# First steps of a one-core decoder layer: x loaded over two queues, squares on two engines, rows scaled in quarters, first casts on GpSimd, four small loads on another queue

## The chip, the core and the metric

The kernel runs on one core of one Trainium2 chip. The metric is the device time of one execution in microseconds (us); the median of the runs is compared. Engines are named as in the profile: PE (TensorE matmuls), PEld (its weight loads), DVE (VectorE), ACT (ScalarE), POOL (GpSimd) and SP (SyncE, which here only starts DMA transfers; its queue is SPq). Line numbers L... are those of the kernel before, unless the text says that they are the changed kernel's.

## What is computed

One decoder layer on x of 256 positions by 1024 channels, in float32. Only the first lines matter here: the row norm of x and the one projection that feeds both mixing branches.

```
def rms_norm(x, g):
    y = xf * lax.rsqrt(jnp.mean(xf * xf, axis=-1, keepdims=True) + NORM_EPS)
    return (y * g.astype(jnp.float32)).astype(x.dtype)
...
        h = rms_norm(x, norm1_g[l])
        proj = h @ w_in[l]
        z_rwkv = proj[..., :RWKV_IN]
...
        z_rwkv = z_rwkv + rwkv_mu[l] * (shift_right(z_rwkv) - z_rwkv)
        y_a = rwkv7_time_mix(z_rwkv, w_decay_up[l], decay_bias[l], w_aaa_up[l], aaa_bias[l],
...
        x = x + (g_a * u_a + g_b * u_b) @ w_out[l]
        h2 = rms_norm(x, norm2_g[l])
        x = x + conv_ffn(h2, w_ffn_up[l], ffn_conv_w[l], ffn_conv_b[l], w_ffn_down[l])
```

After the projection come an RWKV-7 branch (a recurrence over the positions) and a softmax attention branch, gates, an output projection and a gated MLP.

## The kernel before

Every product is made in three passes of float32r halves: an operand is split into a high part (a cast to float32r) and a low part (what the cast lost), and high times high, high times low and low times high are added up. For the activations these halves are `hh` and `hl`, for the weights `whi` and `wlo`. Weights come in pieces of 512 KB (128 partitions by 1024 float32) through `load_next`, which starts a DMA on SP's queue into one of four `raw` buffers (the first piece as two halves of 256 KB, the third piece only 128 KB); `split_hi` casts, `split_lo` subtracts and then starts the next load. Four more pieces are loaded ahead into two tiles named `early`. All DMAs that SP or ACT start share eight completion semaphores in turn, so the ninth waits for the first to land before it is started.

`first_steps` (L364) is written out by hand: within it PE, ACT, DVE and Pool run their instructions in the order of the text, while SP's queue is ordered by the scheduler; after it a scheduler orders all engines. Its order is this:

- x, two blocks of 128 rows in halves of 512 columns, is loaded by four DMAs on SP's queue (`load_x`, L81, called at L99), then come five issues for the first four weight pieces and four for the `early` tiles. ACT starts the load of `p0`, the eight rows of norm1_g.
- Eight dummy matmuls (`keep_warm`) run on PE meanwhile. Pool builds the identity matrix and starts eleven of the fifteen small loads (`small_loads`): ten fill the 51 rows of `p1` (rwkv_mu in two loads, decay_bias, aaa_bias, k_k, k_a, r_k, ln_g, ln_b, norm2_g), the eleventh and twelfth are the two halves of `wdu` (w_decay_up and w_aaa_up, 128 KB each), and the last three are gqk (two loads of 32 KB) and the positions. In the profile norm1_g and norm2_g are both shown as `in_norm_g`, and `p0` and `p1` both as `p`.
- For each row block t: ACT squares both halves with a row sum (L396), DVE scales the first sum and adds the epsilon (L399), ACT takes the root (L401), DVE the reciprocal (L402), and the halves are scaled (L408 on DVE; the last half on ACT, L406). PE transposes eight 128x128 tiles per block (L414); between the blocks four dummy matmuls run.
- The first weight piece is cast half by DVE (L432) and half by Pool (L433), and Pool subtracts (L437). ACT makes `hh` out of the transposes (`high`, L419), DVE makes `hl` (`low`, L422), for K = 0 to 7.
- The first projection's 48 matmuls (L461) run in an order of K and pass written out below; then `late_params` transposes `p1` on PE (L158), copies it to `par` on DVE (L159) and derives `omm` from it (L160). ACT's `shift` (L490) of the first projection needs `omm`, and a `tanh` of its result feeds the decay projection (L566), which uses `wdu`.

Behind that the generator `wst` runs the further projections with the matmuls of L302, L304 and L307.

Of the kernel before, what the change touches and what calls it, by code (L numbers as in the profile page):

```python
# [13 lines left out]
OP = mybir.AluOpType  # L14
# [23 lines left out]
def body(tc, x, positions, norm1_g, w_in, rwkv_mu, w_decay_up, decay_bias, w_aaa_up,  # L38
# [5 lines left out]
    with ctx:  # L44
# [36 lines left out]
        def load_x():  # L81
            xs = []
            for t in range(2):
                xt = b4("x").rearrange("p a b -> p (a b)")
                for cs in (slice(0, 512), slice(512, 1024)):
                    nc.sync.dma_start(xt[:, cs], xr[t * 128:(t + 1) * 128, cs])
                xs.append(xt)
            return xs
# [9 lines left out]

        x_sb = load_x()  # L99
# [84 lines left out]
        def small_loads(n):  # L184
            for _ in range(n):
                nc.gpsimd.dma_start(*loads.pop(0))
# [177 lines left out]
        def first_steps():  # L364

            for i in range(NRAW):
# [8 lines left out]
            nc.scalar.dma_start(p0, rows(norm1_g, 8))  # L377
# [4 lines left out]
            small_loads(11)  # L382
# [10 lines left out]
            for t in range(2):  # L393
                xn = [b2("xn1", [128, 512]) for _ in range(2)]
                for hf in range(2):
                    act.activation(xn[hf], x_sb[t][:, hf * 512:hf * 512 + 512], AF.Square,  # L396
                                   accum_out=ss[:, t, hf:hf + 1])
                    if hf == 0:
                        dve.tensor_scalar(ss[:, t, 0:1], ss[:, t, 0:1], 1.0 / D, NORM_EPS,  # L399
                                          op0=OP.mult, op1=OP.add)  # L400
                act.activation(rs[:, t:t + 1], ss[:, t, 1:2], AF.Sqrt, scale=1.0 / D, bias=ss[:, t, 0:1])  # L401
                dve.reciprocal(rs[:, t:t + 1], rs[:, t:t + 1])  # L402
                for hf in range(2):
                    src = x_sb[t][:, hf * 512:hf * 512 + 512]
                    if t and hf:
                        act.activation(xn[hf], src, AF.Copy, scale=rs[:, t:t + 1])  # L406
                    else:
                        dve.tensor_scalar(xn[hf], src, rs[:, t:t + 1], None, op0=OP.mult)  # L408
                if t == 0:
                    pe.transpose(pt[:, 0:8], p0, ident[:8, :8])  # L410
                    keep_warm(3)
                    dve.tensor_copy(par[:, 0:8], pt[:, 0:8])
                for k in range(8):
                    pe.transpose(at(k)[:, t], xn[k // 4][:, k % 4 * 128:k % 4 * 128 + 128], ident)  # L414
# [961 lines left out]
```

## Time and profile before

| what | value |
|---|---|
| median of 3 runs (lowest, highest) | 406.03 us (405.90, 407.27) |
| span of the profiled execution | 403.9 us |
| median above that span | 2.1 us |
| PE busy | 396.4 us, 98% of the span |
| DVE, ACT, POOL busy | 324.6, 233.9, 41.8 us |
| DMA moved | 70.53 MB, mean 175 GB/s |

The span is from the first to the last instruction of the one execution that was profiled; for that execution no time beside the span is recorded, so the 2.1 us are the distance between it and the median of the other runs. A row of the timeline has the start and the length in us, the engine, the line, the operation, the tiles written and read, the shape and the count of merged instructions; behind it in brackets stands how long the engine sat idle before it and what ended that. A DMA row has the transfer, the issuing queue, the count, KB each and the us from issue to landing. `x4` behind a row means that four instructions were merged, and its length is that of all of them.

### The profile page before, as it was taken

How to read it: one execution, taken by the hardware profiler on the slowest of the kernel's cores; microseconds unless marked ns; L12 is line 12 of the kernel's file. 1: busy time of each engine (PE TensorE's matmuls, PEld its weight loads, DVE VectorE, ACT ScalarE, POOL GpSimd, SP SyncE). 2: the span in 40 equal slices, each digit the busy share in tenths (PEclk: the TensorE clock that was granted, in tenths of full speed). 3: DMA queues.
4: the chain of work that ended last, by engine and by line, in shares of the span. 5: the costliest groups of instructions: out<-in, count | busy, mean ns of one | idle time of the engine just before them, and what ended most of it. 6: DMA issues, size and time to landing. Idle time of an engine off the chain costs nothing.

```text
span 403.9 us, 8280 instructions
## 1 busy us (share of the span) xinstructions
PE 396.4 (98%) x3250; PEld 348.7 (86%) x3250; DVE 324.6 (80%) x574; ACT 233.9 (58%) x397; POOL 41.8 (10%) x69
## 2 busy tenths in 40 slices
PE   7999999999989999999999999999999999999996
PEld 3999989788989989999888888888888888888885
DVE  3988999899667978778965898977869778687694
ACT  6799755475647676444563784655546446355440
POOL 7910070010500011020011000000000000000000
PEclk9999999999999999999999999999999999999999
DMA  8954555564783444536563756676665665656612
GB/s 243 317 168 154 160 161 158 160 176 150 159 220 104 115 150 131 183 112 207 191 183 97 242 157 208 181 232 189 200 204 163 208 187 177 207 174 209 196 48 104
DMA packets 61990, 70.53 MB, mean 175 GB/s; under 512 B 9421, under 2 KB 52243, under 8 KB 61952
## 3 DMA queue, kind: packets, MB, share of 16 engines
q1 hardware_dynamic: 61104, 69.54, 57.1%
q0 software_dynamic: 832, 0.47, 0.6%
q8 instruction: 25, 0.41, 0.5%
q14 instruction: 13, 0.11, 0.1%
q10 hardware_dynamic: 16, 0.00, 0.0%
HBM read 68.56 MB, written 1.44 MB: 173 GB/s over the span
## 4 chain that ended last, share of the span: by engine, by line
PE 93%; DVE 2%; ACT 1%; DMA 1%; issue 1%; SPq 0%; POOL 0%; DVEq 0%; POOLq 0%; ACTq 0%
PE acc L1262 15%; PE acc L302 9%; PE acc L304 8%; PE acc L307 8%; PE acc L1267 8%; PE at L1262 5%; PE acc L323 5%; PE acc L327 5%; PE acc L324 5%; PE f L1286 5%; PE f L1282 5%; PE f L1284 4%; PE at L1267 3%; PE acc L461 1%; DMA x<-in_x_dram 1%; PE pgr L682 1%
## 5 line engine op out<-in xcount | busy, mean ns | idle before, releaser
L259 ACT CAST whi<-raw 128x1024 fp32r<-128x1024 f32 x120 | 125.7, 1051 | 106.0 <-PE acc L1262 22.2
L269 DVE TENSOR_TENSOR wlo<-raw,whi 128x1024 fp32r<-128x1024 f32 x121 | 148.8, 1234 | 26.2 <-PE acc L1267 12.2
L1262 PE MATMUL acc<-hx,whi 128*128 128x512 f32 x264 | 68.2, 393 | 0.0
L302 PE MATMUL acc<-hx,whi 128*128 128x256 f32 x232 | 58.3, 287 | 0.0
L304 PE MATMUL acc<-hx,whi 128*128 128x256 f32 x232 | 55.9, 277 | 0.0
L1262 PEld LDWEIGHTS acc<-hx,whi 128*128 128x128 f32 x264 | 47.0, 188 | 8.1
L302 PEld LDWEIGHTS acc<-hx,whi 128*128 128x128 f32 x232 | 43.6, 188 | 2.0 <-issue 0.8
L304 PEld LDWEIGHTS acc<-hx,whi 128*128 128x128 f32 x232 | 43.6, 188 | 0.1
L1267 PEld LDWEIGHTS acc<-h,wlo 128*128 128x128 f32 x264 | 37.1, 188 | 3.6
L1267 PE MATMUL acc<-h,wlo 128*128 128x256 f32 x264 | 37.8, 279 | 0.0
L307 PE MATMUL acc<-hx,wlo 128*128 128x256 f32 x232 | 35.7, 277 | 0.0
L1284 PE MATMUL f<-whi,hb 128*128 128x512 f32 x80 | 31.2, 390 | 0.0
L1286 PE MATMUL f<-wlo,hb 128*128 128x512 f32 x80 | 31.2, 390 | 0.0
L1282 PE MATMUL f<-whi,hb 128*128 128x512 f32 x80 | 31.2, 389 | 0.0
L307 PEld LDWEIGHTS acc<-hx,wlo 128*128 128x128 f32 x232 | 30.6, 188 | 0.0
L1262 PE MATMUL at<-hx,whi 128*128 128x512 f32 x88 | 24.0, 392 | 0.0
L1272 DVE TENSOR_REDUCE an<-acc 128x256 f32<-128x512 f32 x22 | 14.2, 685 | 9.3 <-PE acc L1267 9.3
L1262 PEld LDWEIGHTS at<-hx,whi 128*128 128x128 f32 x88 | 16.4, 188 | 3.6
L323 PE MATMUL acc<-whi,hx 128*128 128x512 f32 x48 | 19.1, 399 | 0.0
L324 PE MATMUL acc<-whi,hx 128*128 128x512 f32 x48 | 18.8, 391 | 0.0
L1286 PEld LDWEIGHTS f<-wlo,hb 128*128 128x128 f32 x80 | 15.0, 188 | 3.2
L1284 PEld LDWEIGHTS f<-whi,hb 128*128 128x128 f32 x80 | 15.0, 188 | 2.8
(331 smaller groups left out, 688.5 us busy)
## 6 DMA issues: line engine op xcount, KB each, us to landing
raw<-in_w_ffn_up_dram SPq DMA_DIRECT2D x44, 512.0 KB, 4.3
raw<-in_w_in_dram SPq DMA_DIRECT2D x37, 512.0 KB, 4.3
raw<-in_w_ffn_down_dram SPq DMA_DIRECT2D x22, 512.0 KB, 4.0
raw<-in_w_out_dram SPq DMA_DIRECT2D x8, 512.0 KB, 4.1
x<-in_x_dram SPq DMA_DIRECT2D x8, 256.0 KB, 4.4
early<-in_w_in_dram SPq DMA_DIRECT2D x4, 512.0 KB, 7.6
raw<-in_w_branch_b_dram SPq DMA_DIRECT2D x4, 512.0 KB, 3.4
raw<-in_w_branch_a_dram SPq DMA_DIRECT2D x4, 512.0 KB, 3.5
```

Source lines behind the costliest of these rows:

```text
L259: act.copy(wide(hi, k, c), spread(raw, k, c))
L269: eng.tensor_tensor(wide(lo, k, c), spread(raw, k, c), wide(hi, k, c).bitcast(F32), op=OP.subtract)
L302: pe.matmul(om, wh[:, k, ms], xh[:, k0 + k], start=k0 + k + m == 0, stop=False, skip_group_check=True)
L304: pe.matmul(om, wh[:, k, ms], xl[:, k0 + k], start=False, stop=False, skip_group_check=True)
L307: pe.matmul(om, wl[:, k, ms], xh[:, k0 + k], start=False, stop=k0 + k == nk - 1 and m == n - 1, skip_group_check=True)
L323: pe.matmul(ps_[t], xh[:, K, ts], wh[:, k], start=K == 0, stop=False)
L324: pe.matmul(ps_[t], xl[:, K, ts], wh[:, k], start=False, stop=False)
L1262: pe.matmul(ps_[m], wh[:, k, m * 128:m * 128 + 128], hx[:, k0 + k].rearrange("p a s -> p (a s)"), start=k0 + k == 0, stop=False, skip_grou ...
L1267: pe.matmul(ps_[m][:, 0:S], wl[:, k, m * 128:m * 128 + 128], h2[k0 // 4][:, k], start=False, stop=k0 + k == 7, skip_group_check=True)
L1282: pe.matmul(fin[f], hb[:, 0, i, ts], wh[:, 0, cs], start=st, stop=False, skip_group_check=f == 3)
L1284: pe.matmul(fin[f], hb[:, 1, i, ts], wh[:, 0, cs], start=False, stop=False, skip_group_check=f == 3)
L1286: pe.matmul(fin[f], hb[:, 0, i, ts], wl[:, 0, cs], start=False, stop=False, skip_group_check=f == 3)
```

## The change

It touches the first steps alone.

- x's four DMAs are started inside `first_steps`; the second half of block 0 goes over ACT's queue, and SP starts the other three. `p0` follows on ACT's queue.
- Of the small loads Pool starts eight at first (not eleven). ln_b, norm2_g and both halves of `wdu` are started on SP's queue, ahead of the first reuse of a `raw` buffer; the last three stay with Pool.
- The squares of a block's first half stay on ACT (scaled by 1/32 before, the epsilon added by a small ACT instruction), those of the second half go to DVE as one multiply with a row sum.
- Block 0's first half is scaled by DVE and its second by ACT; block 1 is scaled by DVE in four quarters of 256 columns. The transposes run in the order t0 k0-3, t1 k0-1, t0 k4-7, t1 k2-7. The four dummy matmuls between the blocks are gone.
- Both halves of the first weight piece are cast by Pool.
- The first projection begins with the two high passes of K=0 and 1, then their low passes.

```
-        def load_x():
+        def load_x(second):
...
-                for cs in (slice(0, 512), slice(512, 1024)):
-                    nc.sync.dma_start(xt[:, cs], xr[t * 128:(t + 1) * 128, cs])
+                for eng, cs in ((nc.sync, slice(0, 512)), (nc.sync if t else second, slice(512, 1024))):
+                    eng.dma_start(xt[:, cs], xr[t * 128:(t + 1) * 128, cs])
...
-        def small_loads(n):
+        def small_loads(n, eng=nc.gpsimd):
             for _ in range(n):
-                nc.gpsimd.dma_start(*loads.pop(0))
+                eng.dma_start(*loads.pop(0))
...
+            x_sb = load_x(nc.scalar)
+            nc.scalar.dma_start(p0, rows(norm1_g, 8))
             for i in range(NRAW):
                 load_next(i == 0)
             for t in early:
...
-            nc.scalar.dma_start(p0, rows(norm1_g, 8))
...
-            small_loads(11)
+            small_loads(8)
...
+            def squares(t):
+                dst, src = row(t, 0, 512)
+                act.activation(dst, src, AF.Square, scale=1.0 / 32, accum_out=ss[:, t, 0:1])
+                act.activation(ss[:, t, 0:1], ss[:, t, 0:1], AF.Identity, bias=eps1[:, 0:1])
+                dst, src = row(t, 512, 512)
+                dve.scalar_tensor_tensor(dst, src, 1.0 / D, src, op0=OP.mult, op1=OP.mult, accum_out=ss[:, t, 1:2])
+
+            def root(t):
+                act.activation(rs[:, t:t + 1], ss[:, t, 1:2], AF.Sqrt, bias=ss[:, t, 0:1])
+                dve.reciprocal(rs[:, t:t + 1], rs[:, t:t + 1])
...
+            pe.transpose(pt[:, 0:8], p0, ident[:8, :8])
+            keep_warm(3)
+            squares(0)
+            root(0)
+            squares(1)
+            scaled(0, 0, 512)
+            dve.tensor_copy(par[:, 0:8], pt[:, 0:8])
+            root(1)
+            dst, src = row(0, 512, 512)
+            act.activation(dst, src, AF.Copy, scale=rs[:, 0:1])
+            for c in range(0, 1024, 256):
+                scaled(1, c, 256)
+            turn(0, 0, 4)
+            turn(1, 0, 2)
+            turn(0, 4, 8)
+            turn(1, 2, 8)
...
-            dve.tensor_copy(hi[:, hs[0]], raw[:, hs[0]])
-            pool.tensor_copy(hi[:, hs[1]], raw[:, hs[1]])
+            for i in range(2):
+                pool.tensor_copy(hi[:, hs[i]], raw[:, hs[i]])
...
+            small_loads(4, nc.sync)
             load_next()
             small_loads(len(loads))
...
-            both(0, 4)
+            first(0, 0, hh)
+            first(1, 0, hh)
+            first(0, 0, hl)
+            first(1, 0, hl)
+            both(2, 4)
```

What this makes of the queues, in the order in which the program has them. First SP's queue from its start: before,

```order
L86 DMA x<-in_x_dram 128x512 x4
L236 DMA raw<-in_w_in_dram 128x2x256 x2
L236 DMA raw<-in_w_in_dram 128x4x256
L236 DMA raw<-in_w_in_dram 128x8x32
L236 DMA raw<-in_w_in_dram 128x4x256
L236 DMA early<-in_w_in_dram 128x4x256 x4
L236 DMA raw<-in_w_in_dram 128x4x256 x3
```

and now:

```order
L86 DMA x<-in_x_dram 128x512 x3
L234 DMA raw<-in_w_in_dram 128x2x256 x2
L234 DMA raw<-in_w_in_dram 128x4x256
L234 DMA raw<-in_w_in_dram 128x8x32
L234 DMA raw<-in_w_in_dram 128x4x256
L234 DMA early<-in_w_in_dram 128x4x256 x4
L184 DMA p_70<-in_rwkv_ln_b_dram 4x128
L184 DMA p_70<-in_norm_g_dram 8x128
L184 DMA wdu<-in_w_decay_up_dram 64x512
L184 DMA wdu<-in_w_aaa_up_dram 64x512
L234 DMA raw<-in_w_in_dram 128x4x256 x3
```

One transfer of x has left the front, and the four small loads stand behind the four `early` loads. The names `p_70` and `p_69` are `p1` and `p0`. Second, PE's row around the transpose of `p1` (L158 before, L156 now): before,

```order
L461 MATMUL acc<-hx,whi 128x256 x8
L302 MATMUL acc<-hx,whi 128x256
L304 MATMUL acc<-hx,whi 128x256
L302 MATMUL acc<-hx,whi 128x256
L304 MATMUL acc<-hx,whi 128x256
L461 MATMUL acc<-hx,wlo 128x256 x8
L158 MATMUL pt<-ident,p_70 128x51
L302 MATMUL acc<-hx,whi 128x256
```

and now:

```order
L477 MATMUL acc<-hx,whi 128x256 x8
L477 MATMUL acc<-hx,wlo 128x256 x8
L156 MATMUL pt<-ident,p_70 128x51
L300 MATMUL acc<-hx,whi 128x256
L302 MATMUL acc<-hx,whi 128x256
```

Four matmuls of the next projection stood ahead of the transpose and stand behind it now. Third, Pool's row from the last of the `p1` loads on: before,

```order
L186 DMA p_70<-in_rwkv_ln_g_dram 4x128
L186 DMA p_70<-in_rwkv_ln_b_dram 4x128
L186 DMA p_70<-in_norm_g_dram 8x128
L186 DMA wdu<-in_w_decay_up_dram 64x512
L433 CAST whi<-raw 128x512
L437 TENSOR_TENSOR wlo<-raw,whi 128x512 x2
L186 DMA wdu<-in_w_aaa_up_dram 64x512
L186 DMA gqk<-in_q_norm_g_dram 128x64
```

and now:

```order
L184 DMA p_70<-in_rwkv_ln_g_dram 4x128
L448 CAST whi<-raw 128x512 x2
L452 TENSOR_TENSOR wlo<-raw,whi 128x512 x2
L184 DMA gqk<-in_q_norm_g_dram 128x64
```

Pool's two casts follow the eighth small load directly.

More of the change, by code (lines that the diff above doesn't have):

```diff
@@ L97, in body @@
         rk1 = r_k[0].rearrange("h n -> (h n)").rearrange("(n c) -> n c", c=128)
-        x_sb = load_x()
         early = [b8("early", [128, 2, 1024]) for _ in range(2)]
@@ L391, in at @@
                 return pts[min(k, 6)][:, k // 7]
[L393 to L414, printed above, removed]
-                if t == 0:
-                    keep_warm(4)
@@ new lines, in first_steps, with row @@
+            xn = [[b2("xn1", [128, 512]) for _ in range(2)] for _ in range(2)]
+            def row(t, c0, n):
+                return xn[t][c0 // 512][:, c0 % 512:c0 % 512 + n], x_sb[t][:, c0:c0 + n]
+            def squares(t):
[4 more added lines that the diff above has]
+                dve.scalar_tensor_tensor(dst, src, 1.0 / D, src, op0=OP.mult, op1=OP.mult, accum_out=ss[:, t, 1:2])
@@ new lines, in root, with scaled, turn @@
+            def root(t):
+                act.activation(rs[:, t:t + 1], ss[:, t, 1:2], AF.Sqrt, bias=ss[:, t, 0:1])
+                dve.reciprocal(rs[:, t:t + 1], rs[:, t:t + 1])
+            def scaled(t, c0, n):
+                dst, src = row(t, c0, n)
+                dve.tensor_scalar(dst, src, rs[:, t:t + 1], None, op0=OP.mult)
+            def turn(t, k0, k1):
+                for k in range(k0, k1):
+                    pe.transpose(at(k)[:, t], row(t, k * 128, 128)[0], ident)
+            pe.transpose(pt[:, 0:8], p0, ident[:8, :8])
@@ L1189, in body @@
                 threads.remove(th)
-        x_sb = load_x()
+        x_sb = load_x(nc.sync)
         p2 = t1("p2", (88, 128))
```

## The prediction

> **What bounds the kernel now.** The page's head, engine table and chain come first: they say which engine the end hangs on.
> ```profile
> span 403.9 us, 8280 instructions
> PE 396.4 (98%) x3250; PEld 348.7 (86%) x3250; DVE 324.6 (80%) x574; ACT 233.9 (58%) x397; POOL 41.8 (10%) x69
> PE 93%; DVE 2%; ACT 1%; DMA 1%; issue 1%; SPq 0%; POOL 0%; DVEq 0%; POOLq 0%; ACTq 0%
> ```
> TensorE (PE) is busy for 396.4 of 403.9 us and carries 93% of the chain, so only 7.5 us are idle at all. The busy time of stretches (length, PE, weight load, DVE, ACT, POOL, clock, DMA share, GB/s) says where.
> ```profile
> 0.00:5.00 5.00, 3.54 (x9) 1.04 (x9) 0.79 (x12) 2.66 (x5) 4.20 (x14) 1.00 0.59 178
> 5.00:10.00 5.00, 4.28 (x26) 2.68 (x26) 2.49 (x10) 3.66 (x11) 3.56 (x7) 1.00 1.07 305
> 10.00:15.00 5.00, 4.98 (x44) 4.78 (x44) 4.46 (x10) 4.39 (x10) 5.00 (x7) 1.00 1.11 307
> 15.00:20.00 5.00, 5.00 (x42) 4.73 (x41) 5.00 (x10) 2.93 (x6) 4.77 (x11) 1.00 1.11 328
> 30.00:50.00 20.00, 20.00 (x211) 18.98 (x210) 17.98 (x26) 17.55 (x27) 0.00 (x0) 1.00 0.53 159
> ```
> From 10 us PE does not stop, and the DMA engines are full from 5 to 20 us (share 1.07 to 1.11). So the change can move only the moment from which PE runs without a hole; what it moves there is carried to the end nearly whole. The chain in order of time (start, length, what) tells what sets that moment.
> ```profile
> 2.12 4.97 DMA x<-in_x_dram
> 8.93 1.09 PE xt L414 x8
> 10.34 4.59 PE acc L461 x38
> 16.47 0.19 PE pt L158
> 16.66 0.31 PE acc L302
> 18.24 0.91 PE acc L307 x8
> ```
> In the timeline of PE, the same place reads so (start, length):
> ```profile
> 9.82 2.39 PE L461 MATMUL acc<-hx,whi 128*128 128x256 f32 x16
> 16.40 0.26 PE L158 MATMUL pt<-ident,p 51*128 51x51 f32 x1
> ```
> The last quarter of x lands at 2.12 + 4.97 = 7.09 us, the second row block's transposes follow at 8.93, the first projection's 48 matmuls run from 9.82, and L158 comes behind them at 16.40. L158 is the transpose of p1, the small parameters: PE works in order, so whatever p1 lacks there stops everything behind it. A 256-column matmul costs 0.91 / 8 = 0.114 us.
>
> **The front: x, squares, scaling, casts.** The pieces of the old and new front have these prices.
> ```profile
> 3.44 0.63 ACT L396 ACTIVATE xn<-x 128x512 f32<-128x512 f32 x1 [0.59 <-DMA x<-in_x_dram]
> 6.63 0.21 DVE L146 TENSOR_REDUCE rowf<-ident 128x1 f32<-128x64 f32 x1
> 6.76 0.16 DVE L412 COPY par<-pt 128x8 f32<-128x8 f32 x1
> 8.19 0.16 DVE L402 RECIPROCAL rs<-rs 128x1 f32<-128x1 f32 x1 [1.21 <-ACT rs L401]
> 8.39 0.49 DVE L408 TENSOR_SCALAR xn<-x,rs 128x512 f32<-128x512 f32 x1
> 9.80 1.66 DVE L422 SCALAR_TENSOR_TENSOR hx<-xt,par,hx 128x256 fp32r<-128x256 f32 x4 [0.59 <-ACT hx L419]
> 9.66 0.61 POOL L433 CAST whi<-raw 128x512 fp32r<-128x512 f32 x1
> 10.24 2.73 POOL L437 TENSOR_TENSOR wlo<-raw,whi 128x512 fp32r<-128x512 f32 x2
> ```
> x: SyncE issues one transfer fewer ahead of the last quarter, 0.47 us by the distance of two issues (2.12 to 2.59 in the trace). If the transfer engines and not the issue set the landing, nothing is gained; I take 0.2 of 0 to 0.47. The Trainium skill (DMA: Bandwidth & Descriptors, "Issuing engines are not separate DMA queues") says that starting transfers from several engines only saves the issuing time. By that rule x gains at most those 0.47 us, not half of the load.
>
> So the last quarter lands at about 6.9. From there the new order on VectorE (DVE) is: square of that half (no row; 0.63 as on ACT to 0.83 as two of L422, I take 0.8), first half of block 0 scaled 0.49, L146 0.21, par 0.16, reciprocal 0.16, four quarters of block 1 at some 0.27 each (half of 0.49 plus start) 1.1, and then the last four transposes, 4/8 of 1.09, 0.5: the first matmul at 6.9 + 3.4 = 10.3, against 9.82 before. The square root on ACT (0.3) lies beside the scaling. Pool now does both casts, 2 x 0.61, ahead of its subtractions (2.73 for two). It has three issues fewer in front of them, but even if it began only at the old cast's 9.66, the first half of wlo would be there at 9.66 + 1.22 + 1.37 = 12.25, and PE asks for it at 10.3 + 16 x 0.114 = 12.1: hidden, or 0.15 us late at worst.
>
> The new order has both high passes of K=0,1 ahead of the low ones, which removes holes: before, 52 matmuls (48 and four of the next group) took 16.40 - 9.82 = 6.6 us against 52 x 0.114 = 5.9. Without holes 48 take 5.5, and the new kernel is at its p1 transpose at 10.3 + 5.5 = 15.8. The four matmuls that stood ahead of it now stand behind; without them the old one was there at 16.40 - 4 x 0.114 = 15.95. So the front alone is worth 0.15 us, between -0.6 (later) and +0.6.
>
> **The four moved loads.** ln_b and norm2_g, rows of p1, and the two halves of wdu leave Pool's queue for SyncE's, where they stand behind the four "early" weight loads. Today they go like this (issue; then size and us to landing):
> ```profile
> 6.66 0.52 POOL L186 DMA_DIRECT2D p<-in_rwkv_ln_b_dram  x1 [0.18 <-issue]
> 8.32 0.65 POOL L186 DMA_DIRECT2D p<-in_norm_g_dram  x1 [1.15 <-DMA p<-in_rwkv_mu_dram]
> p<-in_norm_g_dram POOLq DMA_DIRECT2D x1, 4.0 KB, 4.7
> wdu<-in_w_decay_up_dram POOLq DMA_DIRECT2D x1, 128.0 KB, 6.0
> ```
> p1 is whole at 8.32 + 4.7 = 13.0, over 3 us before PE asks. Now the queue that they are moved to: issues of the first, second and last early load, and the time to landing of the first, second and last.
> ```profile
> 7.17 1.70 SPq L236 DMA_DIRECT2D early<-in_w_in_dram  x1
> 8.91 1.05 SPq L236 DMA_DIRECT2D early<-in_w_in_dram  x1
> 10.56 0.53 SPq L236 DMA_DIRECT2D early<-in_w_in_dram  x1
> early<-in_w_in_dram SPq DMA_DIRECT2D x1, 512.0 KB, 7.2
> early<-in_w_in_dram SPq DMA_DIRECT2D x1, 512.0 KB, 7.4
> early<-in_w_in_dram SPq DMA_DIRECT2D x1, 512.0 KB, 9.8
> ```
> They land at 14.4, 16.3 and 20.4, in the order of their issue and about 2 us apart: the queue is a line of work 7 us long. A small load issued at 11 us behind the last of them should land when they have, not 5 us later. When is that in the new kernel? From 20.4 comes off what is no longer ahead of it: the 256 KB of wdu, 0.26 MB at the 351 GB/s of the first row here, 0.75 us; and the dents that these loads made:
> ```profile
> 11.00:12.00 1.00, 1.00 (x11) 1.00 (x10) 1.00 (x4) 1.00 (x4) 1.00 (x2) 1.00 1.10 351
> 13.00:14.00 1.00, 1.00 (x12) 1.00 (x11) 0.46 (x3) 0.92 (x2) 1.00 (x2) 1.00 1.04 199
> 18.00:19.00 1.00, 1.00 (x12) 1.00 (x11) 1.00 (x4) 0.47 (x1) 1.00 (x2) 1.00 1.07 297
> ```
> (351 - 199) / 351 = 0.43 us and (351 - 297) / 351 = 0.15. With 0.2 from x, 20.4 - 0.75 - 0.43 - 0.15 - 0.2 = 18.9. That is the last share of a 512 KB load; a load of 4 or 8 rows need not wait for the slowest share. The mean one comes out of the bytes: x, five weight issues and four early loads are 4736 KB, 4.85 MB, with the 0.33 MB of wdu and gqk from Pool 5.18 MB; the windows moved 0.89 + 1.53 + 1.54 = 3.95 MB by 15 us, and the rest at 328 GB/s ends at 18.75, less the same 1.53 us: 17.2. So p1 is whole between 17.0 (x gains all 0.47) and 19.1 (x gains nothing); between the two ends I take 18.2, a little nearer the measured landing.
>
> PE stands at its p1 transpose from 15.8 to 18.2, and the front's cost no longer counts: the hole hides it. Against the old 15.95 the shift is 18.2 - 15.95 = **+2.25 us** (+1.05 to +3.15). Behind the transpose DVE is held too: par's copy (now right behind PE, before 1 us later) and with it the next weight cast, omm, and so ACT's first shift. Those start some 1.3 us behind p1 and the decay projection needs them 33 matmuls later (3.8 us): covered. wdu follows p1 by 256 KB, 0.75 us: covered too. The next weight load waits on Pool no longer (13.0 before) but on a landing of the early loads, 14 us; what it brings is used past 30 us, where PE is full and the DMA share is 0.53: covered. Nothing later gives the hole back, since PE is full until 50 us in the rows above.
>
> Sum on the profiled run: 403.9 + 2.25 = 406.15 us of span. The median of the runs, 406.03, is 2.1 above that span, so **408.3 us**.
>
> **Rivals.** *In time:* the small loads don't stand in line (they slip through, or the line is 2 us shorter than I reckon), so p1 is there by 15.8. For it: they are 6 KB. Against: early loads that land in issue order. Then only the front counts, 406.03 - 0.15 = 405.9 (405.4 to 406.6), no change.
>
> *The clock falls in the hole:* PE begins slow and needs work to get up to pace.
> ```profile
> 1.46 3.59 PE L109 MATMUL idle<-ones 128*128 128x512 bf16 x8 [1.46 <-DVE eps L374]
> 7.31 1.03 PE L109 MATMUL idle<-ones 128*128 128x512 bf16 x4
> ```
> Eight in 3.59 us are some 0.43 apart, four in 1.03 some 0.22. The new hole of 2.4 us could bring the slow pace back for about 4 us, 2 us lost: 410.3. It decides from a hole that is long enough; no row of before has such a hole, and the granted clock reads 1.00 throughout, even in the slow stretch. The Trainium skill (TensorE: Matmul & The Clock Gate, "What's actually happening") has the clock halved after an idle window of about 3.4 us. By that rule this hole is too short unless p1 comes after 19.2. The removed four fillers leave a second gap, 6.3 to about 8, ahead of the transposes; what it cost would lie under the wait for p1.
>
> *Faster by more than 2 us:* the front would have to give more than its own holes (0.7) and the x issue (0.47); I see no such mechanism.
>
> **How the numbers follow.** A measurement of this kernel can tell about 0.5%, 2.0 us. Late p1: 0.75, of which 0.46 over 2.0 us (p1 past 18.0) and 0.29 below. In time: 0.13. Clock: 0.09. Faster: 0.03. So slower 0.46 + 0.09 = 0.55, same 0.29 + 0.13 = 0.42, faster 0.03. Late p1 has the range 407.1 to 409.2; with most of "in time" and its upper end stretched towards the clock case, 405.4 to 409.6.
>
> **What would show it.** Right: PE idle ahead of the 51-row transpose, released by a DMA of norm2_g or ln_b, for about 2.4 us; these two with over 6 us to landing from SyncE; the first weight matmul at about 10. Wrong: PE at that transpose with no wait; half-pace matmuls behind it; or a hole that the middle of the kernel gives back.

## The result, and the profile after

The changed kernel takes 411.12 us (median of 6 runs, 409.90 to 412.61), the kernel before 406.03 (405.71 to 407.37): a ratio of 1.012, 95% interval 1.0087 to 1.0153. The direction was forecast, the size was not: +5.1 us against +2.25, past the end of the range. The profiled execution is the longest of the six, 412.61 us with this span:

```profile
span 410.7 us, 8276 instructions
PE 400.3 (97%) x3246; PEld 350.5 (85%) x3246; DVE 328.5 (80%) x577; ACT 233.7 (57%) x395; POOL 38.2 (9%) x66
```

PE is busy 3.9 us longer although it has four matmuls fewer. The stretches of the start (columns as in the prediction; the granted clock is the third number from the end):

```profile
5.00:10.00 5.00, 2.79 (x14) 1.38 (x14) 2.94 (x9) 2.33 (x7) 3.59 (x6) 1.00 1.06 319
10.00:15.00 5.00, 3.69 (x17) 2.59 (x16) 5.00 (x9) 3.28 (x8) 4.94 (x9) 0.52 1.10 349
15.00:20.00 5.00, 5.00 (x38) 5.00 (x37) 4.46 (x7) 3.82 (x5) 2.78 (x17) 0.80 1.12 265
20.00:25.00 5.00, 5.00 (x44) 4.69 (x44) 4.12 (x9) 1.54 (x5) 0.00 (x0) 1.00 0.99 324
```

Before, PE was busy 4.98 of the 5 us from 10 to 15 at clock 1.00. Now it is busy 3.69, at a granted clock of 0.52. The chain says what it was waiting for:

```profile
1.64 5.53 DMA x<-in_x_dram
...
9.02 4.04 DVE xn L410 x4
...
13.80 7.03 PE acc L477 x48
20.82 0.19 PE pt L156
```

x lands at 7.17, as late as before (7.09), so in this pair of traces the second queue gave nothing. Executions differ, though: the last quarter of x was taken up between 6.04 and 7.46 us in the 13 traces of this case with two queues (mean 6.56), and between 6.19 and 7.92 in the seven with one (mean 7.03). Then come two terms that the forecast had small: the four quarter scalings of block 1 (4.04 us, forecast 1.1) and the 48 matmuls (7.03, forecast 5.5). VectorE and Pool side by side, VectorE first (the first row is the first quarter alone, the second all four together, the third the last one alone):

```profile
9.02 0.35 DVE L410 TENSOR_SCALAR xn<-x,rs 128x256 f32<-128x256 f32 x1
9.02 4.03 DVE L410 TENSOR_SCALAR xn<-x,rs 128x256 f32<-128x256 f32 x4
11.84 1.21 DVE L410 TENSOR_SCALAR xn<-x,rs 128x256 f32<-128x256 f32 x1
```

```profile
7.82 1.36 POOL L448 CAST whi<-raw 128x512 fp32r<-128x512 f32 x2 [1.34 <-DMA raw<-in_w_in_dram]
9.15 2.62 POOL L452 TENSOR_TENSOR wlo<-raw,whi 128x512 fp32r<-128x512 f32 x2
11.71 0.62 POOL L184 DMA_DIRECT2D gqk<-in_q_norm_g_dram  x1
12.33 0.54 POOL L184 DMA_DIRECT2D gqk<-in_k_norm_g_dram  x1
```

One quarter takes 0.35 us, four took 4.03. The second and third end 0.15 us behind the ends of Pool's two subtractions (some 1.3 us each): each seems to sit through a whole instruction of Pool. The last one starts when the subtractions are done, at 11.77, and still takes 1.21 us; it ends 0.17 us behind the second of Pool's two issues for gqk. So Pool's starting of small loads seems to hold VectorE as well. PE's timeline at the same time:

```profile
8.77 1.66 PE L414 MATMUL xt<-ident,xn 128*128 128x128 f32 x10 [2.12 <-DVE xn L410]
13.45 3.72 PE L477 MATMUL acc<-hx,whi 128*128 128x256 f32 x16
17.01 0.64 PE L477 MATMUL acc<-hx,wlo 128*128 128x256 f32 x4
20.75 0.26 PE L156 MATMUL pt<-ident,p 51*128 51x51 f32 x1
```

Before, with four dummy matmuls ahead of it, the gap ahead of the second block's transposes was 0.60 us and not 2.12:

```profile
8.93 1.09 PE L414 MATMUL xt<-ident,xn 128*128 128x128 f32 x8 [0.60 <-DVE xn L408]
```

The first 16 matmuls take 17.01 - 13.45 = 3.56 us, 0.22 apiece where 0.114 is the full pace; at 17.0 full pace is back. PE reaches p1's transpose at 20.75 and does not wait for p1. Against 15.95 that is +4.8. Against the forecast's own 15.8 it is 4.95: 2.9 from the quarters (4.03 for 1.1), 1.7 from the half pace, 0.3 from x (7.17 for 6.9). The two loads for p1 do stand where the change put them, behind the early loads:

```profile
10.90 0.47 SPq L184 DMA_DIRECT2D p<-in_rwkv_ln_b_dram  x1
11.42 0.28 SPq L184 DMA_DIRECT2D p<-in_norm_g_dram  x1
```

So the predicted hole is not in this trace: p1 was whole before the late front got there. And there is a third thing, at the other end of the kernel. Matmul by matmul the distance to before is 4.8 us from 25 to 110 us and 5.0 at 221, but then it grows: 5.3 at 261, 5.8 at 322, 6.4 at 382. The growth sits in one group, the products with `hb` as weights (the down projection). Before, then after, grouped by line (count, busy us, mean ns):

```profile
L1282 PE MATMUL f<-whi,hb 128*128 128x512 f32 x80 | 31.2, 389 | 0.0
```

```profile
L1302 PE MATMUL f<-whi,hb 128*128 128x512 f32 x80 | 31.6, 395 | 0.0
```

264 such matmuls at 6 ns more are 1.6 us. Their code was not touched. What was: `load_x` now takes its two tiles from the pool behind `early`, so the buffers of that size, `hb`'s among them, lie elsewhere in SBUF (the first `hb` at byte 152960 before, at 193952 now).

### The profile page after: what moved, and what is told of

Same layout as the page of the kernel before. It is cut to its first block, busy times and chain, and to the rows that moved or that the text cites. A ratio compares the mean times of both kernels' runs of the same rounds, so it can differ in the third digit from the quotient of the medians.

```text
span 410.7 us, 8276 instructions
## 1 busy us (share of the span) xinstructions
PE 400.3 (97%) x3246; PEld 350.5 (85%) x3246; DVE 328.5 (80%) x577; ACT 233.7 (57%) x395; POOL 38.2 (9%) x66
## 4 chain that ended last, share of the span: by engine, by line
PE 94%; DVE 2%; DMA 1%; issue 1%; ACT 0%; POOL 0%; SPq 0%; POOLq 0%
PE acc L1282 15%; PE acc L300 9%; PE acc L302 8%; PE acc L305 8%; PE acc L1287 7%; PE at L1282 5%; PE acc L321 5%; PE f L1304 5%; PE f L1306 5%; PE f L1302 5%; PE acc L325 4%; PE acc L322 4%; PE at L1287 2%; PE acc L477 2%; DMA x<-in_x_dram 1%; DVE xn L410 1%
## 5 line engine op out<-in xcount | busy, mean ns | idle before, releaser
L257 ACT CAST whi<-raw 128x1024 fp32r<-128x1024 f32 x120 | 125.8, 1051 | 109.6 <-PE acc L1282 20.3
L267 DVE TENSOR_TENSOR wlo<-raw,whi 128x1024 fp32r<-128x1024 f32 x121 | 148.6, 1232 | 29.5 <-PE acc L1287 10.7
L1304 PE MATMUL f<-whi,hb 128*128 128x512 f32 x80 | 31.7, 396 | 0.0
L1302 PE MATMUL f<-whi,hb 128*128 128x512 f32 x80 | 31.6, 395 | 0.0
L321 PE MATMUL acc<-whi,hx 128*128 128x512 f32 x48 | 19.1, 399 | 0.0
```

Of the source, the lines that this page charges most:

```text
L257: act.copy(wide(hi, k, c), spread(raw, k, c))
L267: eng.tensor_tensor(wide(lo, k, c), spread(raw, k, c), wide(hi, k, c).bitcast(F32), op=OP.subtract)
L321: pe.matmul(ps_[t], xh[:, K, ts], wh[:, k], start=K == 0, stop=False)
L1302: pe.matmul(fin[f], hb[:, 0, i, ts], wh[:, 0, cs], start=st, stop=False, skip_group_check=f == 3)
L1304: pe.matmul(fin[f], hb[:, 1, i, ts], wh[:, 0, cs], start=False, stop=False, skip_group_check=f == 3)
```

## The experiments

Four causes are held against each other: **lock** (VectorE's quarters wait for Pool), **clock** (half pace behind a gap that fillers used to cover), **late p1** (the prediction), **addresses** (where `hb` lies). All results, against the kernel before as it ran beside them (its medians were 405.8 for e1 to e4, 405.9 for e5 to e8, 406.1 for e9 to e12, 406.2 for the rest). The ratio is an estimate from the runs of both kernels and not the quotient of the two medians:

| run | edit in short | median us | ratio (95%) |
|---|---|---|---|
| e1 | changed, fillers back | 416.06 | 1.0245 (1.0207, 1.0283) |
| e2 | changed, scalings in another form | 412.31 | 1.0172 (1.0122, 1.0222) |
| e3 | both | 415.14 | 1.0243 (1.0190, 1.0296) |
| e4 | e3, p1's loads on ScalarE's queue | 416.65 | 1.0258 (1.0221, 1.0295) |
| e5 | e3, order mended | 413.98 | 1.0172 (1.0121, 1.0222) |
| e6 | e4, order mended | 410.40 | 1.0071 (1.0038, 1.0104) |
| e7 | before, the four loads moved | 411.46 | 1.0110 (1.0068, 1.0152) |
| e8 | changed, p1's loads on ScalarE's queue | 409.22 | 1.0077 (1.0050, 1.0105) |
| e9 | changed, x tiles in their old places | 409.38 | 1.0086 (1.0064, 1.0108) |
| e10 | before, x tiles in their new places | 407.35 | 1.0046 (1.0026, 1.0066) |
| e11 | before without the four fillers | 406.62 | 1.0017 (0.9992, 1.0043) |
| e12 | e7, fillers ahead of p1's transpose | 411.39 | 1.0125 (1.0085, 1.0166) |
| e13 | e8 and e9 | 407.47 | 1.0038 (1.0017, 1.0059) |
| e14 | e13 and e2 | 407.95 | 1.0054 (1.0028, 1.0079) |
| e15 | e9 and e6 | 407.34 | 1.0034 (1.0011, 1.0057) |
| e16 | before, K order, aligned b2 | 405.71 | 1.0009 (0.9986, 1.0033) |
| e17 | changed, 32 bytes of padding | 411.77 | 1.0143 (1.0099, 1.0186) |
| e18 | before, 32 bytes of padding | 407.82 | 1.0038 (1.0019, 1.0056) |

**e1, fillers.** Eight more dummy matmuls ahead of the transposes and eleven between them.

```
-            keep_warm(3)
+            keep_warm(11)
...
             turn(0, 4, 8)
-            turn(1, 2, 8)
+            keep_warm(3)
+            turn(1, 2, 4)
+            keep_warm(4)
+            turn(1, 4, 6)
+            keep_warm(4)
+            turn(1, 6, 8)
```

> The changed kernel with dummy matmuls in PE's gaps of the first steps (8 more ahead of the transposes, 11 between them), nothing else. Theory A (three costs: DVE's quarter scalings wait for Pool, PE falls to half pace, p1 comes late and is hidden behind both): the first weight matmul stays at about 13.4 us, because the quarters still take 4 us, but the 48 matmuls take 5.5 us instead of 7.3, so PE is at p1's transpose at about 19 instead of 20.8. Of the six runs of the changed kernel about half show the low clock, so the median falls by 0.9 to 1.8: 409.3 to 410.2. Rival B (the clock does not matter, the late front is one chain on DVE): no change, 411.

PE's timeline, then VectorE's:

```profile
12.41 2.13 PE L482 MATMUL acc<-hx,whi 128*128 128x256 f32 x16
19.85 0.68 PE L482 MATMUL acc<-hx,whi 128*128 128x256 f32 x2 [2.72 <-DVE hx L442]
```

```profile
18.81 0.17 DVE L192 CAST posf<-posi 128x2 f32<-128x2 int32 x1 [3.89 <-DMA posi<-in_positions_dram]
```

The 16 matmuls are back at 2 us, so the half pace came from the gap (further down this is seen in six traces with fillers). But the time rose, from 411.12 to 416.06, where 409.3 to 410.2 was expected: in the order that the scheduler made with the fillers, VectorE has a cast of the positions ahead of the last low part, and that cast waits 3.89 us for a DMA that has nothing to do with the front. PE stands behind it. As a test of the sum the run is spoiled; it shows the clock's part alone.

**e2, the scalings in a form that also writes a sum.** Same arithmetic, same order of all engines.

```
-dve.tensor_scalar(dst, src, rs[:, t:t + 1], None, op0=OP.mult)
+dve.tensor_scalar(dst, src, rs[:, t:t + 1], 0.0, op0=OP.mult, op1=OP.add, accum_out=junk1[:, 0:1])
```

> The changed kernel, only that the five row scalings on DVE also write a sum that nobody reads, so that they run in another form of the same operation. Theory A, by the Trainium skill (SBUF - State Buffer, Who interferes with whom): the plain form takes the port pair shared with GpSimd and waits for a whole GpSimd instruction, the form with a sum does not. So the four quarters take 0.4 to 0.5 us each, 1.8 in all, not 4.0, though Pool casts and subtracts beside them; the first weight matmul comes at about 11.2 instead of 13.4, and p1, landing at about 18.6, then ends the wait ahead of its transpose: 409 to 410. Rival C (a piece of 256 columns takes 1 us at that time for another reason, such as the full transfer engines): the quarters stay at about 1 us and the time at 411.

The first and the third quarter on VectorE, Pool's subtractions beside them, then PE:

```profile
9.14 0.48 DVE L411 TENSOR_SCALAR_CACHE_REDUCE xn<-x,rs 128x256 f32<-128x256 f32 x1
10.19 0.48 DVE L411 TENSOR_SCALAR_CACHE_REDUCE xn<-x,rs 128x256 f32<-128x256 f32 x1
9.58 2.51 POOL L453 TENSOR_TENSOR wlo<-raw,whi 128x512 fp32r<-128x512 f32 x2
```

```profile
11.95 2.83 PE L478 MATMUL acc<-hx,whi 128*128 128x256 f32 x16
20.62 0.24 PE L156 MATMUL pt<-ident,p 51*128 51x51 f32 x1 [2.08 <-DMA p<-in_norm_g_dram]
```

In this form each quarter takes 0.48 us (and 0.08 to read the sum) right beside Pool's subtractions; the four are done in 2.1 us instead of 4.03. That is the lock shown: same data, same neighbour, another form of instruction. The Trainium skill (SBUF — State Buffer, "Who interferes with whom") says that VectorE in its two-port modes and Pool share a pair of ports which the first to come holds for its whole instruction, and that the form that also writes its accumulator does not take them; 1.3 us against 0.48 agrees. The time did not fall, because p1 now stands behind it: PE waits 2.08 us for norm2_g. p1 lets PE go at 20.62 here, just ahead of the 20.75 at which the changed kernel's PE got there, so the predicted hole seems to have lain under the slower front.

**e3, e4, e5, e6: front cured, p1 late or early.** e3 has e2's form and the fillers (eleven ahead, two between the transposes), e4 also moves the two loads:

```
-            small_loads(4, nc.sync)
+            small_loads(2, nc.sync)
...
             nc.scalar.dma_start(p0, rows(norm1_g, 8))
+            for _ in range(2):
+                nc.scalar.dma_start(*loads.pop(8))
```

> Both: the form with a sum for the row scalings, and 10 more dummy matmuls (8 ahead of the transposes, 2 between). Theory A: with both front costs gone PE is at p1's transpose at 16 to 17 us and stands there until p1 is whole at 18.4 to 18.8, the hole of the prediction: 2 to 2.7 us over before, 408.0 to 408.8. Rival D (p1's landing does not matter at all): PE goes through its transpose without a wait and the time is at 406 to 407.

> As the one with both front costs gone, and ln_b and norm2_g are started on ACT's queue right behind p0 instead of on SP's behind the early loads. Theory A: p1 is whole before 10 us, no wait at its transpose, and the time is 405.7 to 407.0, 1.5 to 2.7 below the kernel with both front costs gone alone. Rival D: the same time as that one.

Both fell into e1's trap: the cast of the positions waited 4.08 and 7.02 us on VectorE, and PE stood for 3.49 and 6.34 us behind it. For e5 and e6, and all later runs that say so, the cast and a scaling of a mask are held behind the third cast of an early tile, where the kernel before and the changed one have them anyway:

```
+            with tc.issue_after(dcast[2]):
+                dve.tensor_copy(posf, posi)
```

> The changed kernel with the row scalings in the form with a sum and 10 dummy matmuls (8 ahead of the transposes, 2 between), and two small DVE instructions of the next stage (the positions' cast and a mask's scaling) held behind the third early cast, where the kernels before and after have them; in the first try of this edit the scheduler had put them ahead of the last low part, which then waited for the positions. Theory A (Pool's lock, clock, p1 late and hidden behind both): PE is at p1's transpose at 16 to 17 us and waits there until p1 is whole at 18.5 to 20.5: 2.3 to 4.5 us over before, 408.2 to 410.5. Rival D (p1's landing costs nothing): 406 to 407.

> The same, and ln_b and norm2_g on ACT's queue behind p0. Theory A: p1 is whole by about 5 us plus Pool's rows by 11, no wait at its transpose, 405.7 to 407.0, and 2 to 4 below the same kernel with these two loads on SP's queue. Rival D: no difference between the two.

PE in e5, then in e6:

```profile
10.73 2.12 PE L482 MATMUL acc<-hx,whi 128*128 128x256 f32 x16
19.66 0.23 PE L157 MATMUL pt<-ident,p 51*128 51x51 f32 x1 [2.32 <-DMA p<-in_norm_g_dram]
21.40 0.42 PE L305 MATMUL acc<-hx,whi 128*128 128x256 f32 x1
```

```profile
10.35 2.12 PE L484 MATMUL acc<-hx,whi 128*128 128x256 f32 x16
16.31 0.26 PE L157 MATMUL pt<-ident,p 51*128 51x51 f32 x1
```

With the front at the forecast pace (first matmul at 10.4 to 10.7, forecast 10.3) e5 has the forecast hole, 2.32 us long, and behind it, from 21.2 us, matmuls of 0.21 us apiece: the rival "the clock falls in the hole". With p1 on ScalarE's queue (e6) PE is at the transpose at 16.31 and does not wait; the distance to before is 0.25 us from 24 to 100 us, inside the -0.6 to +0.6 that the prediction gave the front alone.

Both medians missed what was expected: 413.98 against 408.2 to 410.5 (e5), 410.40 against 405.7 to 407.0 (e6). e5's trace is 5.2 us behind before at 24 us, 2.8 more at 221 us (in between the granted clock is 0.50 from 127.0 to 130.4 us), and 1.6 more at the end, from the `hb` products. e6's trace is one of its fastest executions (408.54); it loses 0.8 us more by 221 us and the same 1.6. Why five of its eight executions took 410.3 us or more is not shown.

**e7, the four loads alone.** The kernel before, ln_b, norm2_g and wdu on SyncE's queue behind the early loads (order held as in e5).

```
-            small_loads(11)
+            small_loads(8)
...
+            small_loads(4, nc.sync)
             load_next()
```

> The kernel before with one part of the change alone: ln_b, norm2_g and both halves of wdu on SP's queue behind the early loads (Pool starts eight small loads first and so gets to its cast earlier). Theory A, the prediction's step by itself: p1 is whole at 18 to 20.5 us, PE waits for it with nothing to hide it, 2 to 4 us over before: 408 to 410. Rival D: within 0.5 us of before.

The issue on SyncE's queue, PE, and a stretch:

```profile
11.52 0.28 SPq L187 DMA_DIRECT2D p<-in_norm_g_dram  x1
```

```profile
15.49 1.09 PE L465 MATMUL acc<-hx,wlo 128*128 128x256 f32 x8
18.66 0.23 PE L159 MATMUL pt<-ident,p 51*128 51x51 f32 x1 [2.07 <-DMA p<-in_norm_g_dram]
20.25 1.91 PE L310 MATMUL acc<-hx,wlo 128*128 128x256 f32 x8
```

```profile
19.85:23.20 3.35, 3.35 (x18) 3.35 (x17) 2.05 (x5) 1.48 (x4) 0.27 (x3) 0.50 1.11 354
```

This is the prediction's case without its front: 4 KB take 7.1 us from issue to use, p1's transpose stands at 18.66 against 16.40, +2.26, where the prediction said +2.25. That they agree so closely is luck: six matmuls of the next projection stand ahead of the transpose here, where before it was four, and in e12, the same kernel but for four dummy matmuls, p1 lets PE go only at 20.27. And eight matmuls behind it take 1.91 us instead of 1.09: from 19.85 to 23.20 the granted clock is 0.50, and half of 3.35 us is 1.7 more. The distance settles at 4.2 us and stays there to the end of the kernel. In this trace late p1 costs twice what its hole shows, and it is the fastest of the four runs: the median, 411.46, is 5.6 us above before's, past the 408 to 410 expected. So p1's loads alone are enough to make the kernel before as slow as the changed one.

**e8, p1's loads on ScalarE's queue.** The changed kernel with e4's edit alone (order held).

> The changed kernel with ln_b and norm2_g on ACT's queue behind p0, nothing else. Theory A: DVE's waits for Pool and PE's half pace keep PE busy up to its p1 transpose until 19 to 20.8 us, so that p1 in time is worth 0 to 1.5 us: 409.6 to 411. Rival P (p1 late is the main cost of the change): 406 to 408.5.

1.9 us less than the changed kernel. In its profile the quarters ran nearly free:

```profile
7.68 1.14 DVE L415 TENSOR_SCALAR xn<-x,rs 128x256 f32<-128x256 f32 x4
```

Here x landed at 6.3, and the second half of the first weights only at 9.0, so Pool was waiting when VectorE scaled: no lock. Half pace is there all the same, from 8.2 to 11.6 us. How much of the 1.9 us is p1's wait and how much the lock can't be told from one trace; such landings differ by up to 1.7 us between executions (x, in the same place of the same queue, was taken up at 6.19 us in e7 and at 7.92 in e10).

**e9 and e10, places.** e9 is the changed kernel with the x tiles taken from their pool ahead of `early` and still loaded where the change loads them; e10 is the kernel before with `load_x` called where the change calls it, all on SyncE's queue. No instruction or transfer changes its place in either.

```
+        x_t = [b4("x") for _ in range(2)]
+
         early = [b8("early", [128, 2, 1024]) for _ in range(2)]
...
-            x_sb = load_x(nc.scalar)
+            x_sb = load_x(nc.scalar, x_t)
```

```
-        x_sb = load_x()
-
         early = [b8("early", [128, 2, 1024]) for _ in range(2)]
...
+            x_sb = load_x()
             for i in range(NRAW):
```

> The changed kernel with one edit: the two x tiles are taken from their pool where the kernel before took them, ahead of the early tiles; every transfer and instruction stands where the change put it. In the kernel before, the buffer of hb starts at SBUF address 152960, a multiple of 64; in the changed one at 193952, 32 past one, and its 264 matmuls with hb as weights took about 395 ns against 389. Theory 'addresses': the FFN's growth of the shift (1.3 to 1.6 us between 240 and 400 us) is these 264 x 6 ns and comes from the 32 bytes. The f matmuls fall back to 389 ns, the shift stays constant from 225 us to the end, and the time is about 1.5 us below the changed kernel's, 409.6. Rival 'order': the growth comes from the new front by some other way (transfers or clock late in the kernel); nothing changes, 411.1, and f stays at 395 ns.

> The kernel before with one edit: the x tiles are taken from their pool where the change takes them, behind the early tiles, so that hb starts 32 bytes past a multiple of 64; the order of all instructions and transfers is that of before. Theory 'addresses': the f matmuls rise from 389 to 395 ns, the shift against before grows by 1.3 to 1.6 us between 240 and 400 us, 407.4 in all. Rival 'order': no change, 405.9, f at 389 ns.

The `hb` products by line, e9 and e10:

```profile
L1304 PE MATMUL f<-whi,hb 128*128 128x512 f32 x80 | 31.2, 389 | 0.0
```

```profile
L1281 PE MATMUL f<-whi,hb 128*128 128x512 f32 x80 | 31.6, 395 | 0.0
```

Both came out as "addresses" said, in both directions: 409.38 against 409.6 forecast, 407.35 against 407.4; in e9 the distance to before is 3.71 us from 241 to 382 us without growth, in e10 it grows by 1.3.

**e11 and e12, gaps.** e11 is the kernel before without the four fillers between the blocks, e12 is e7 with four dummy matmuls ahead of p1's transpose (order held in both).

```
-                if t == 0:
-                    keep_warm(4)
```

```
+            for _ in range(4):
+                pe.matmul(pt, ones[:, 0:128], ones, start=True, stop=True)
             pe.transpose(pt[:, 0:51], p1, ident[:51, :51])
```

> The kernel before with one edit: the four filler matmuls between the two row blocks' transposes are left out (two setup instructions pinned to their old place in VectorE's order). The gap ahead of block 1's transposes grows from 0.6 to about 1.6 us. Theory 'clock': a gap of 1.6 us is shorter than those of 2.07 to 2.3 us behind which matmuls ran at half pace; if transposes count as work it stays at full pace, 406; if transposes do not count, TensorE has had no work that counts from 6.5 to 9.8 us (3.3 us), half pace follows for about 3.4 us, and the time is 1.7 to 2 us longer, 407.8. Rival 'fillers are idle talk': 405.9 with the granted clock at 1.00 throughout.

> The kernel with the four loads alone moved to SyncE's queue, and four dummy matmuls of 128x512 (0.87 us in all) ahead of the transposition of p1, so that the hole there shrinks from 2.07 us to about 1.2 us; a few instructions of the time behind 25 us change places by the scheduler's reckoning. Theory 'two parts': p1's landing costs 18.66 - 16.40 = 2.26 us, and the half pace that follows the hole (19.85 to 23.2 us) the other 2 us of that kernel's 4.2; with the shorter hole the clock stays at 1.00, the shift at 25 us is 2.3 to 2.5, and the time 408.2. Rival 'one part': the hole's length does not matter or 1.2 us is enough; half pace remains, shift 3.6 to 4.2 us, 410.1.

PE in e11, then in e12:

```profile
9.53 1.09 PE L417 MATMUL xt<-ident,xn 128*128 128x128 f32 x8 [2.00 <-DVE xn L411]
10.43 2.44 PE L462 MATMUL acc<-hx,whi 128*128 128x256 f32 x16
```

```profile
16.67 1.04 PE L160 MATMUL pt<-ones 128*128 128x512 bf16 x3
20.27 0.31 PE L161 MATMUL pt<-ident,p 51*128 51x51 f32 x1 [2.57 <-DMA p<-in_norm_g_dram]
```

In e11 a gap of 2.00 us left the pace whole, and the ratio's interval holds 1: the fillers alone are worth nothing here that can be measured. The trace, of the slowest of its ten runs, does have half pace elsewhere, from 124.9 to 128.3 us; that this has to do with the fillers is not shown. e12 told nothing about a shorter hole: p1 came 1.6 us later than in e7 and the hole was 2.57 us long in spite of the fillers, with half pace behind it.

**e13, e14, e15: the cures in steps.** e13 joins e8's and e9's edits, e14 adds e2's form, e15 adds e3's fillers (order held in all three).

> The changed kernel with ln_b and norm2_g on ScalarE's queue behind norm1_g (wdu stays on SyncE's) and the x tiles at their old addresses. Theory 'sum': p1's 1.9 us (409.22 against 411.12) and the addresses' 1.4 us (407.35 against 406.07 and 411.12 against 409.38) add: 407.7, 0.4% above before; what is left is the front, +0.9 us at 24 us and +0.9 us at 225 us, constant behind that. Rival 'cover': with p1 out of the way the front's own losses (quarters behind Pool, half pace) come to light in full, 409 or more.

> The kernel with p1 on ScalarE's queue and the x tiles at their old addresses, and the row scalings in the form that also writes a sum (two inputs' worth of work: 0.48 + 0.08 us a quarter beside Pool, where the plain form takes 0.35 alone and up to 1.36 beside Pool). Theory 'lock': where the first weights land before the last quarter of x, the plain quarters take 4 us in all and these 2.2; where they land after, 1.1 and 2.2. In the kernel it is compared with, the quarters took 1.14 us in its profile, so the form can cost up to 1.1 us or gain up to 1.8: 406.8 to 408.5, with first matmul at about 11.2 us in any execution. Rival: the lock's price is the same in each execution, and curing it gains 1.5 to 3 us: 405 to 406.

> All cures in one: p1 on ScalarE's queue, row scalings in the accumulating form, fillers ahead of and between the transposes (eleven and two), x tiles at their old addresses. Theory 'sum': without the addresses' 1.4 to 1.6 us the front-cured kernel with p1 on ScalarE's queue (408.7 by its ratio, shift 0.25 us at 24 us, 1.1 at 225) stands at 407.1 to 407.3, and the FFN's f matmuls at 389 ns; half pace shows nowhere. Rival 'something else is left': above 408.

VectorE and PE in e13, then PE in e14 and in e15:

```profile
8.21 2.51 DVE L417 TENSOR_SCALAR xn<-x,rs 128x256 f32<-128x256 f32 x4
```

```profile
11.29 3.37 PE L484 MATMUL acc<-hx,whi 128*128 128x256 f32 x16
```

```profile
10.02 2.08 PE L485 MATMUL acc<-hx,whi 128*128 128x256 f32 x16
```

```profile
10.57 2.12 PE L486 MATMUL acc<-hx,whi 128*128 128x256 f32 x16
```

In e13 most of the first 16 matmuls run at 0.21 us apiece, up to 13.9 us, although the granted clock reads 1.00 there, as it does in the slow matmuls at the kernel's start; this half pace is read off the spacing. Over all traces of the changed front, the 16 matmuls run at full pace in the six with fillers (e1, e3 to e6, e15), and at half pace, in part or whole, in six of the seven without (the changed kernel, e2, e8, e9, e13, e17; not in e14).

"Sum" held: 407.47 against 407.7 forecast, and e15 407.34. Curing the lock and the half pace as well moved the median by no more than the runs scatter (+0.5, -0.1), though the traces show it done: the sum-writing form costs 2.1 us in every trace, the plain one 1.1 to 4.0 by who lands first. What is left, 1.1 to 1.5 us, was not removed by any cure; e15's trace has 1.2 of it at 24 us and 0.6 more between 100 and 150 us, and it was not taken apart further.

**e16, the other side.** The kernel before with the change's order of K (both high passes first) and 32 bytes ahead of the b2 buffers (order as before).

```
-            both(0, 4)
+            first(0, 0, hh)
+            first(1, 0, hh)
+            first(0, 0, hl)
+            first(1, 0, hl)
+            both(2, 4)
...
+            pad = sb.tile([128, 8], F32, name="padb")
             ss = sb.tile([128, 2, 2], F32, name="ss1")
```

> The kernel before with two edits: both high passes of K=0,1 ahead of their low passes, as in the change, and 32 bytes of padding ahead of the b2 buffers, so that every operand of TensorE starts at a multiple of 64. The first removes holes of up to 0.6 us between 9.8 and 16.4 us; the second takes up to 6 ns off some 100 matmuls with weights from b2, 0.6 us at most. Theory: 0.3 to 1.2 us less than before, 405.3. Rival: the holes are given back at p1 or in the stage from 110 to 140 us, no change, 406.0.

405.71 us: no difference that can be measured. Its trace is ahead by 0.3 us at 24 us and 0.6 from 125 us on, within what executions of one kernel differ.

**e17 and e18, 32 bytes.** One tile of 32 bytes ahead of the x tiles; in e18 a second one behind them.

```
+            pad = sb.tile([128, 8], F32, name="pad")
             x_sb = load_x(nc.scalar)
```

> The changed kernel with 32 bytes of padding ahead of the x tiles: hb starts at 193984, a multiple of 64, 32 bytes behind the changed kernel's 193952; the order of all instructions is the changed kernel's. Theory '32 bytes': the f matmuls fall from 395 to 389 ns and the time by about 1.5 us, to 409.5. Rival 'place': they stay at 395 ns, 411.1.

> The kernel before with 32 bytes of padding ahead of the x tiles (and 32 behind them): hb starts at 152992, 32 past a multiple of 64, in the old place but for these bytes; the order of all instructions is that of before. Theory '32 bytes': the f matmuls rise from 389 to 395 ns and the time by 1.3 to 1.6 us, to 407.5. Rival 'place': 389 ns and 406.1.

By line, and one row of PE's timeline in e17:

```profile
L1303 PE MATMUL f<-whi,hb 128*128 128x512 f32 x79 | 31.2, 394 | 0.0
```

```profile
20.50 0.24 PE L156 MATMUL pt<-ident,p 51*128 51x51 f32 x1 [0.55 <-DMA p<-in_norm_g_dram]
```

And e18:

```profile
L1284 PE MATMUL f<-whi,hb 128*128 128x512 f32 x80 | 31.6, 395 | 0.0
```

e18 shows that 32 bytes are enough to cost 1.7 us in a layout in which nothing else moved by more than 64. e17 refutes the rule that went with it: at 193984, a multiple of 64, the products stay slow. The four places tried are fast at 152960 (e9 too), a multiple of 128, and slow at 152992, 193952 and 193984, which are 32, 32 and 64 past one. A start at a multiple of 128 fits all four, but was read off afterwards and not tested. e17 also shows how close the two covers lie: with quarters of 3.53 us PE waited 0.55 us for p1.

## Why the prediction was wrong

- **The step that failed is the front**: "the front alone is worth 0.15 us, between -0.6 (later) and +0.6", from "four quarters of block 1 at some 0.27 each" and "48 take 5.5". In the profile the quarters took 4.03 and the matmuls 7.0, and PE came 4.8 us late. Its durations were measured with VectorE alone and with PE at full pace; the change moved Pool's two casts and its subtractions under the quarters and opened a gap of 2.12 us. The prediction costed Pool's casts as "hidden, or 0.15 us late", asking when Pool would be done and not what Pool would do to its neighbour. With p1 and the places cured, what is left of the change still costs 0.7 to 2.4 us (e13's interval), past the bound. That this rest is the lock and the half pace is not shown: curing both as well took nothing measurable off it (e15), so it stays open.
- **"The hole hides it" was the wrong way round**: in the profiled execution the front hid the hole. The sum took the front's cost as covered by p1; each covers the other, and which ends last changes with the landings (0.55 us of wait in e17, none in the profile).
- **Late p1 was right in place and cause, too small in size.** Wherever the front was on time, the hole stood there (e2, e5, e7). But p1 let PE go at 18.7, 19.7, 20.3, 20.5 and 20.6 us in e7, e5, e12, e17 and e2, where 17.0 to 19.1 was given; e7's 2.26 us, so close to the forecast 2.25, belong to the earliest of the five. And the hole was priced at its length alone; e7's trace lost 4.2 us, its median 5.6.
- **Half pace was a rival with 0.09 and came often**: behind p1's hole in e5, e7 and e12 (not in e2), behind the transposes' gap in the profile. Its price of 2 us was about right (1.7 in e7). The chance was too low because "no row of before has such a hole" was read as evidence against it. The second gap, ahead of the transposes, was seen and put under the wait for p1, where it was not.
- **The places were not thought of at all**: "PE is full" was taken to mean that nothing later changes. 264 matmuls got 6 ns longer each, 1.3 to 1.7 us by e9, e10 and e18, a third of the loss; no view of the profile before shows it, but the moved call to `load_x` was in the diff.
- x over two queues gave nothing in the two profiles (7.17 against 7.09) and 0.47 us in the mean of all traces (6.56 against 7.03), both inside the 0 to 0.47 given. The new order of K has no holes, as said, but it is worth nothing that can be measured (e16).

Put together: 1.7 us for the places (e9 against the changed kernel), 1.9 for p1's loads (e8; e13 against e9 again 1.9), and some 1.3 for the rest (e13 against before) make 4.9 of the 5.1. The three are steps of one chain, from the changed kernel over e9 and e13 to before, so that they add up proves nothing by itself; what bears them out is e8 for p1's loads, and e10 and e18 for the places (1.3 and 1.7). The price of p1's loads also depends on the front: 1.9 us under the late one, 4.2 or more without it (e7).

## What to carry to other kernels

Before a duration from an old trace goes into a sum, ask what will run beside it in the new order: work moved to an idle Pool is not free if VectorE runs plain scalings next to it. A wait on the busiest engine costs its length and possibly a stretch at half pace behind it, so price both; one trace shows one landing, so ask several for its spread; and where two late things lie on top of each other, cure both before judging either. A moved tile allocation is a change by itself: compare a group of untouched instructions far from the edit, and keep the old places when only the order is meant to change.

## What the runs showed of the hardware

- A plain VectorE scaling of 128x256 took 0.35 us, about 1.3 us beside Pool's subtractions, and 1.21 us beside Pool's starting of two small loads; with a written sum 0.48 + 0.08 us beside the subtractions.
- By the granted clock, half pace came in stretches of 3.41 us or twice that: 19.86 to 23.27 us in e7, 20.14 to 23.55 in e12, 10.17 to 17.00 in the changed kernel. Holes of nearly the same length had different sequels: half pace from 1.2 us behind a hole of 2.07 us (e7), none behind 2.08 (e2) or 2.00 (e11).
- Where a hole falls explains the difference. Cut each of the 20 traces into stretches of 3.41 us in line with its own half pace. Of those at full pace, all ten in which PE was idle for 1.79 us or more were followed by half pace, three of the seven with 1.45 to 1.77 us, and none of the other 2320, with 1.37 us at most. e7's hole lay whole in one stretch (16.45 to 19.86), e2's with only 1.77 us (16.90 to 20.31). This was read off the traces afterwards; no run tests it.
- The Trainium skill (TensorE: Matmul & The Clock Gate, "What's actually happening") has windows of about 3.4 us that run freely, and a halved clock after an idle one. The 3.4 us and the chance where a hole falls agree. Only e4's hole of 6.34 us filled a window (15.22 to 18.64, with half pace behind it); in the other cases idling for about half of one, or a little more, was enough.
- A matmul of 128x512 with its weights in SBUF took 389 ns from a start at a multiple of 128 bytes and 394 to 396 from 32 or 64 past one.
